# A fixed, software-pipelined order on three engines for the second part of a feed-forward up projection

## The chip, the cores and the metric

The kernel runs on one core of one Trainium2 chip. The metric is device time in microseconds (us) for one execution, median of the runs shown. Engines are called TensorE (PE in the profile), VectorE (DVE), ScalarE (ACT), GpSimd (POOL) and SyncE (SP, which here only issues transfers). A PE row has one matmul, a PEld row the loading of its weights.

## The reference

One decoder layer in fp32, 512 positions, model width 1024. A mixer comes first (mLSTM heads and a convolution group); the change concerns what follows it, the conditioned convolutional feed-forward network with 2816 hidden channels:

```python
mod = silu(c) @ ada_w + ada_b
sh1, sc1, g1, sh2, sc2, g2 = jnp.split(mod, 6)
...
u = rms_norm(x, ffn_pre_g) * (1.0 + sc2) + sh2
up = causal_dwconv(u @ ffn_up, ffn_conv_w, ffn_conv_b)   # width 3
a, gt = jnp.split(up, 2, axis=-1)
f = (silu(gt) * a) @ ffn_down
x = x + g2 * rms_norm(f, ffn_post_g)
```

## The kernel before

**Products in fp32.** Each fp32 operand is written as the sum of a high part (`h` at the end of a name), which ScalarE rounds off by a copy, and a low part (`l`), the remainder. A product is three matmuls: high by high, high by low, low by high (L188 to L190).

**The up projection** has 22 blocks of 128 hidden channels. A block has an "a" half and a "gate" half, and its weights are a tile of 128 x 2048, loaded by SP into a raw buffer; there are two raw buffers. Blocks 0 to 7 are multiplied plainly. From block 8 on blocks come in pairs, an even block i and the odd block j = i + 1; m = i / 2 counts pairs, m = 4 to 10.

*The even block* is computed with seven products of half size in place of eight (a Strassen-like scheme). Its weights are four quarters of 128 x 512 in the raw buffer: a11, a12, a21, a22, the quarters 0 to 3, each loaded by a DMA of 256 KB (L1064 to L1069). Seven operands are formed: p1 is a11, p2 is a12, p4 is a22; p5, p7, p6 and p3 are sums and differences, which VectorE makes in place (L1093, L1094, L1097 for the first three, L1118 for p3: it puts a12 - a11 into a11). p1, p5, p7 and p6 are multiplied first (`first_products`) into the PSUM banks `upx`, `upz` and `upw`. ScalarE then copies two products to SBUF (both called `p` in rows, L1106 and L1109) and VectorE makes four sums between banks (L1110 to L1113); p2, p3 and p4 are accumulated on top of these (L1086 holds all matmuls of the seven products, 84 of them for a block, 12 a product, each with 256 columns).

*The odd block* is multiplied plainly in two halves, 24 matmuls of 512 columns each (L188 to L190); its raw buffer is the second one.

**Two kinds of split.** `w_split` (p1, p5, p7, p6, p3): ScalarE copies the high part (L170), GpSimd subtracts to get the low part (L171). `added_split` (p2, p4, all quarters of odd blocks): ScalarE writes the high part (L1077) and its negative (L1078), and GpSimd issues a DMA (L1079) that adds the raw quarter to the negative, so that the low part is made by a transfer, which reads the raw buffer.

**What follows a block.** The convolution of width 3 (`conv3`): ScalarE takes the middle tap out of PSUM (L995), VectorE adds two more (L997). For the gate half ScalarE applies Silu (L1141), and VectorE multiplies (L1142) into F, one buffer for each pair. `forms` then prepares the pair's F as operand of the down projection, which uses the seven-product scheme too: four sums and differences on VectorE (L1021 to L1024), two splits by ScalarE and VectorE (L1013, L1014), and two DMAs issued by ScalarE that put the rest aside in DRAM (`g2d`, L1031, L1032). For the first four pairs, m = 0 to 3, the split operands go to DRAM as well ("spilled", `own_d`).

**Beside this**, eight pieces of the modulation (`ada`, 512 KB each) are loaded on ScalarE's queue and summed up on VectorE (L153, L155), two at a time at blocks 4, 8, 12 and 16 (`asides`).

**The down projection** runs over 11 groups, one for each pair, in the order 4 to 10, then the spilled 0 to 3; group numbers in rows (`b_3h`, `wd_1`) count in that order. A group's weights are loaded by SP (`load1`, L1220) into the two raw buffers and two more places (`wdmore`), combined on VectorE and split by ScalarE and VectorE (`forms1`, L1226 to L1230), and one combination is written back to DRAM (`t2d`). SP issues, in this order: the loads of groups 0, 1 and 2; sixteen reloads of spilled operands, 256 KB each (`reload`, L1188); then for each group its write of `t2d`, the load of the group three further on, and a load of what `forms` put aside (L1246).

**Who sets the order.** TensorE and SP work in the order in which the code is written. The instructions of ScalarE, VectorE and GpSimd are ordered by a scheduler of the language, by its own estimates of when data are ready, except inside `in_order()` (L70 to L82), where these three also keep the order of the code. The up projection from block 8 on is not inside such a region before the change.

## Time and profile before

| | |
|---|---|
| time, median of 3 runs | 826.61 us (826.61, 823.62, 826.79) |
| the profiled execution | 830.35 us |
| its span on the core | 828.6 us, mean granted TensorE clock 0.962 |
| bytes moved by DMA | 144.80 MB, mean 175 GB/s over the span |
| first product of block 8 on TensorE | at 506.2 us |
| first product of block 20 | at 675.0 us |
| 497 to 560 us: TensorE busy, granted clock, DMA share | 44.73 us of 63, 0.85, 0.70 |
| 560 to 705 us | 126.03 us of 145, 0.90, 0.62 |
| 705 to 828 us | 107.26 us of 123, 0.94, 0.76 |

The span is the time between the first and the last instruction on the core; the execution's own time has some 1.75 us around it. A row of the trace reads: start and length in us, engine, line, operation, output <- inputs, shapes, count, and in brackets how long the engine stood idle before it and what ended that. In a table by windows each engine has its busy time and, in brackets, its instructions, in the order PE, PEld, DVE, ACT, POOL; behind them stand the granted clock (1.00 is full speed), the busy share of the 16 DMA engines and GB/s. A row "PE upx <- DVE upx: 33.1, 6, 14.1" is the total of waits, their number and the longest.

### The profile page before, as it was taken

Reading aid. Unit: us, or ns where it says so; the run is one execution under the profiler, and the core shown is the slowest. Engines: PE = TensorE matmul, PEld = TensorE weight load, DVE = VectorE, ACT = ScalarE, POOL = GpSimd, SP = SyncE. Lnnn points to the kernel's source line nnn. Section 1 sums busy time; section 2 is a strip of 40 time slices with the busy share of each in tenths; the row PEclk is TensorE's granted clock in tenths of the full one; section 3 lists DMA queues with packets and bytes.
Section 4 is the critical chain, followed back from the end, with each engine's and each line's share of the span. In section 5 each row is a group of like instructions: output and inputs, shape, how many; then the busy total and the mean of one; then the engine's idle time right before and its main releaser. Section 6 shows DMA issues by size and latency. Waiting matters only on the chain.

```text
span 828.6 us, 11531 instructions
## 1 busy us (share of the span) xinstructions
PE 769.2 (93%) x3961; PEld 656.9 (79%) x3961; DVE 642.3 (78%) x1039; ACT 444.9 (54%) x846; POOL 372.9 (45%) x315
## 2 busy tenths in 40 slices
PE   7999999999999999999999999389798896879996
PEld 5788898788888889888899888379787796658885
DVE  6979999999999577378676997565676547479996
ACT  5555375867664566523354447265564654255762
POOL 1049495977986444538234765145453440000001
PEclk9999999999999999999999999598899997979998
DMA  9973223131234524287453456686775871797982
GB/s 332 382 267 103 102 97 107 52 102 51 79 125 150 180 78 156 99 294 269 175 182 136 142 190 153 215 181 121 209 171 159 195 152 48 227 372 249 307 282 101
DMA packets 53119, 144.80 MB, mean 175 GB/s; under 512 B 6050, under 2 KB 7490, under 8 KB 48964
## 3 DMA queue, kind: packets, MB, share of 16 engines
q1 hardware_dynamic: 32724, 100.37, 35.3%
q10 hardware_dynamic: 14288, 32.68, 11.3%
q0 software_dynamic: 6048, 11.01, 7.8%
q8 instruction: 31, 0.51, 0.2%
q14 instruction: 28, 0.23, 0.1%
HBM read 117.42 MB, written 15.61 MB: 161 GB/s over the span
## 4 chain that ended last, share of the span: by engine, by line
PE 56%; DVE 20%; DMA 10%; issue 6%; ACT 4%; POOL 2%; SPq 0%; ACTq 0%; DVEq 0%; POOLq 0%
DVE cv L731 10%; PE up L189 4%; PE up L190 4%; PE up L188 4%; PE p L1314 4%; PE upx L1086 4%; DMA wup_p4l<-wups 3%; PE glu L189 3%; PE glu L188 3%; PE glu L190 3%; DMA wups<-in_w_up 2%; PE glu L316 2%; PE p L189 2%; PE p L188 2%; PE p L190 2%
## 5 line engine op out<-in xcount | busy, mean ns | idle before, releaser
L731 DVE SCALAR_TENSOR_TENSOR cv<-gt,cvw,cv 128x505 f32<-128x505 f32 (+24 forms) x200 | 137.3, 729 | 2.3 <-ACT cv L719 1.1
L685 POOL TENSOR_TENSOR ro2r<-ro2t,mhalf 128x1 f32<-128x1 f32 x1 | 0.6, 561 | 134.5 <-DVE ro2t L683 134.5
L1086 PE MATMUL upx<-u2h,wup_p2h 128*128 128x256 f32 x28 | 11.3, 405 | 37.0 <-DVE upx L1113 33.1
L727 POOL TENSOR_TENSOR cs<-cs,cs 128x510 f32<-128x510 f32 (+3 forms) x32 | 41.9, 1309 | 0.3
L1086 PEld LDWEIGHTS upx<-u2h,wup_p2h 128*128 128x128 f32 x28 | 7.8, 280 | 39.8 <-ACT wup_p5h L170 14.5
L171 POOL TENSOR_TENSOR wup_p5l<-wups,wup_p5h 128x512 fp32r<-128x512 f32 x7 | 9.0, 1292 | 52.3 <-ACT wup_p5h L170 46.1
L155 DVE SCALAR_TENSOR_TENSOR junk<-ada,cb 128x1024 bf16<-128x1024 f32 x20 | 29.0, 1448 | 3.4 <-DMA ada<-in_adaT 3.3
L725 ACT ACTIVATE cs<-gt,cvw 128x511 f32<-128x511 f32 (+4 forms) x40 | 27.4, 716 | 6.2 <-POOL cs L727 3.0
L189 PE MATMUL up<-u2l,wup_0h 128*128 128x512 f32 (+1 forms) x72 | 25.7, 356 | 0.2 <-DVE u2l L910 0.2
L188 PE MATMUL up<-u2h,wup_0h 128*128 128x512 f32 (+1 forms) x72 | 25.6, 356 | 0.0
L190 PE MATMUL up<-u2h,wup_0l 128*128 128x512 f32 (+1 forms) x72 | 25.5, 354 | 0.0
L171 POOL TENSOR_TENSOR wqko_1024l<-wqko,wqko_1024h 128x512 fp32r<-128x512 f32 x12 | 15.5, 1293 | 18.3 <-ACT wqko_1024h L170 12.9
L171 POOL TENSOR_TENSOR wglu_0l<-wglu,wglu_0h 128x512 fp32r<-128x512 f32 x4 | 5.6, 1408 | 40.3 <-PE glu L190 40.2
L155 DVE SCALAR_TENSOR_TENSOR junk<-spare,cb 128x1024 bf16<-128x1024 f32 x12 | 19.2, 1598 | 3.4 <-DMA spare<-in_adaT 3.1
L1013 ACT ACTIVATE fh<-F 128x512 fp32r<-128x512 f32 x11 | 6.9, 628 | 27.3 <-DVE F L1022 14.1
L188 PE MATMUL qko<-uh,wqko_1024h 128*128 128x512 f32 x48 | 20.6, 430 | 0.0
L188 PE MATMUL qko<-uh,wqko_0h 128*128 128x512 f32 x48 | 20.2, 420 | 0.0
L276 DVE SCALAR_TENSOR_TENSOR junk<-ada,cb 128x1024 bf16<-128x1024 f32 x16 | 19.5, 1220 | 0.1
L171 POOL TENSOR_TENSOR wo_512l<-wo,wo_512h 128x512 fp32r<-128x512 f32 x8 | 12.9, 1617 | 13.4 <-ACT wo_512h L170 13.4
L190 PE MATMUL qko<-uh,wqko_1024l 128*128 128x512 f32 x48 | 18.8, 392 | 0.0
L171 POOL TENSOR_TENSOR wqko_0l<-wqko,wqko_0h 128x512 fp32r<-128x512 f32 x12 | 16.6, 1382 | 4.9 <-ACT wqko_0h L170 4.9
L190 PE MATMUL qko<-uh,wqko_0l 128*128 128x512 f32 x48 | 18.8, 391 | 0.0
(1207 smaller groups left out, 3186.8 us busy)
## 6 DMA issues: line engine op xcount, KB each, us to landing
wups<-in_w_up SPq DMA_DIRECT2D x56, 256.0 KB, 5.6
wqko<-in_w_qko SPq DMA_DIRECT2D x12, 1024.0 KB, 4.8
ada<-in_adaT ACTq DMA_DIRECT2D x20, 512.0 KB, 5.2
ada<-in_adaT SPq DMA_DIRECT2D x16, 512.0 KB, 7.4
wo<-in_w_out SPq DMA_DIRECT2D x8, 1024.0 KB, 4.8
wup<-in_w_up SPq DMA_DIRECT2D x8, 1024.0 KB, 5.0
spare<-in_adaT ACTq DMA_DIRECT2D x12, 512.0 KB, 7.2
wd<-in_w_down SPq DMA_DIRECT2D x6, 768.0 KB, 6.6
```

What stands on the lines that cost most here:

```text
L155: t = V.scalar_tensor_tensor(out=junk, in0=r, scalar=1.0, in1=cb, op0=ALU.mult, op1=ALU.mult, accum_out=mod[:, i : i + 1])
L171: (eng or G).tensor_tensor(out=lo[:, :n], in0=src, in1=hi[:, :n].bitcast(F32), op=ALU.subtract)
L188: PE.matmul(ps, a[0], b[0], start=start, stop=False)
L189: PE.matmul(ps, a[0], b[1], start=False, stop=False)
L190: PE.matmul(ps, a[1], b[0], start=False, stop=stop)
L276: V.scalar_tensor_tensor(out=junk, in0=first[k][:, i * D : (i + 1) * D], scalar=1.0, in1=cb, op0=ALU.mult, op1=ALU.mult, accum_out=part[k] ...
L316: PE.matmul(banks0[i], blk(wk, i)[a], u[k][b], start=k == 0 and a == b, stop=False)
L725: S.activation(t[:, d:], cvx[j][:, : T - d], AF.Copy, scale=w(CK - 1 - d))
L727: G.tensor_tensor(out=side[:, d:], in0=side[:, d:], in1=t[:, d:], op=ALU.add)
L731: last_tap[0] = V.scalar_tensor_tensor(out=cp[:, d:], in0=cvx[j][:, : T - d], scalar=w(CK - 1 - d), in1=cp[:, d:], op0=ALU.mult, op1=ALU.add)
L1086: PE.matmul(ps, x, y, start=start and k == 0 and n == 0, stop=stop and k == NT - 1 and n == 2, skip_group_check=True)
L1314: PE.matmul(ps[q], x, y, start=False, stop=m == NM - 1 and i == 2, skip_group_check=True)
```

## The change

The part of the up projection from block 8 on is written out inside an `in_order()` region, in one loop over pairs, so ScalarE, VectorE and GpSimd run it in the order of the code. The loop is pipelined over pairs. In the turn of pair m, the engines other than TensorE and SP do:

1. first half-convolution of the odd block of pair m - 1, then p2's split of block i;
2. Silu and product of that odd block; then p3's split (its difference now has a place of its own, `s4`) and p4's split;
3. `forms` of pair m - 1 (high parts and the DMAs), then the copies and sums between banks for block i, then the low parts of `forms` (`forms_low`);
4. the splits of the second half of odd block j;
5. the first forms (p1, p5, p7, p6) of block i + 2, with the first convolution of block j between them; then the splits of the first half of block j + 2;
6. the sums of two pieces of the modulation and the loads of the next two (pairs 4 to 7, before them two loads ahead of the loop);
7. the two convolutions of block i, its Silu and its product.

SP's loads for the next pair stand in the code behind p4's split: quarters 0 and 1 of block j + 2, then 2, 0, 1, 3 of block i + 2, and later 2 and 3 of block j + 2. Before, they were 0, 2, 3, 1 of an even block, then 0 to 3 of the odd one. The order of TensorE's instructions is the same as before. There are still two raw buffers.

The sixteen reloads are issued by GpSimd instead of SP.

Lines of the changed kernel that the prediction speaks of: L1077 to L1079 and L170, L171, L995, L997 as before; L1094 and L1098 (the in-place sums of `first_forms` for p5 and p6), L1115 to L1118 (sums between banks), L1137 (Silu), L1147 (sum of the modulation), L1274, L1284 and L1300 (the down projection's load, write of `t2d` and load of what was put aside).

The diff, cut to its core:

```diff
@@ forms
+        pairs.append([(slot(f"fh{m}_{n}", F32R), slot(f"fl{m}_{n}", F32R)) for n in range(2)])
+        for (hi, _), z in zip(pairs[m], (F[:, :T], ysum)):
+            S.activation(hi, z, AF.Copy)
...
+    def forms_low(m, F):
+        for (hi, lo), z in zip(pairs[m], (F[:, :T], ysum)):
+            V.tensor_tensor(out=lo, in0=z, in1=hi.bitcast(F32), op=ALU.subtract)
@@ first_forms
-        r = up_load(i, (0, 2, 3, 1))
+        a11, a21, a22 = (quarter(up_raw[i % 2], q) for q in (0, 2, 3))
...
         w.append(w_split(a21, f"wup{i}_p5"))
+        middle()
         w.append(w_split(a11, f"wup{i}_p7"))
@@ last_forms
-        V.tensor_tensor(out=a11, in0=a12, in1=a11, op=ALU.subtract)
-        return [added_split(a12, f"wup{i}_p2"), w_split(a11, f"wup{i}_p3"), added_split(a22, f"wup{i}_p4")]
@@ the loop over pairs, before
-            r, w = first_forms(i)
-            banks = first_products(i, w)
-            z = up_load(j, range(4))
-            pa = plain_half(cvbank(f"up{j}_0"), [added_split(quarter(z, q), f"wup{j}_{q}") for q in range(2)], 0)
-            ja = conv3(pa, j, f"fa{j}")
-            last_products_up(banks, last_forms(i, r))
-            unit_out(i, conv3(banks[0], i, f"fa{i}"), conv3(banks[1], NF + i, f"fg{i}"), F)
-            pg = plain_half(cvbank(f"up{j}_1"), [added_split(quarter(z, q), f"wup{j}_{q}") for q in range(2, 4)], 0)
-            unit_out(j, ja, conv3(pg, NF + j, f"fg{j}"), F)
@@ and now
+    up_load(2 * MS, (0, 2, 3, 1))
+    up_load(2 * MS + 1, range(4))
+    with in_order():
+        fetched = [ada_fetch(40 + n) for n in range(2)]
+        first_forms(2 * MS, lambda: None)
+        halves_w = [added_split(quarter(up_raw[1], q), f"wup{2 * MS + 1}_{q}") for q in range(2)]
...
+            if before is not None:
+                bj, ba, bg = before
+                fg = conv3(bg, NF + bj, f"fg{bj}")
+            V.tensor_tensor(out=s4, in0=a12, in1=quarter(up_raw[0], 0), op=ALU.subtract)
+            late = [added_split(a12, f"wup{i}_p2")]
+            if before is not None:
+                unit_out(bj, ba, fg, Fs[m - 1])
+            late.append(w_split(s4, f"wup{i}_p3"))
+            late.append(added_split(a22, f"wup{i}_p4"))
+            if m + 1 < NM:
+                up_load(j + 2, range(2))
+                up_load(i + 2, (2, 0, 1, 3))
+            if before is not None:
+                forms(m - 1, Fs[m - 1])
+            between(i, *banks)
+            if before is not None:
+                forms_low(m - 1, Fs[m - 1])
...
+            halves_w = [added_split(quarter(up_raw[1], q), f"wup{j}_{q}") for q in range(2, 4)]
+            if m + 1 < NM:
+                up_load(j + 2, range(2, 4))
...
+                first_forms(i + 2, value)
...
+            last_products_up(X, Z, late)
+            pg = plain_half(cvbank(f"up{j}_1"), halves_w, 0)
+            if m + 1 < NM:
+                halves_w = [added_split(quarter(up_raw[1], q), f"wup{j + 2}_{q}") for q in range(2)]
...
+            unit_out(i, conv3(X, i, f"fa{i}"), conv3(Z, NF + i, f"fg{i}"), Fs[m])
+            before = j, ja[0], pg
@@ reload
-                nc.sync.dma_start(z.bitcast(F32), own_d[m][:, (2 * n + e) * T : (2 * n + e + 1) * T])
+                G.dma_start(z.bitcast(F32), own_d[m][:, (2 * n + e) * T : (2 * n + e + 1) * T])
```

More of the change, by code (lines that the diff above doesn't have):

```diff
@@ L1068, in up_load @@
             nc.sync.dma_start(quarter(up_raw[i % 2], q), quarter(w_up[i], q))
-        return up_raw[i % 2]
     def quarter(r, b):
@@ L1086, in form_product, with first_forms @@
                 PE.matmul(ps, x, y, start=start and k == 0 and n == 0, stop=stop and k == NT - 1 and n == 2, skip_group_check=True)
-    def first_forms(i):
-        r = up_load(i, (0, 2, 3, 1))
-        a11, a21, a22 = quarter(r, 0), quarter(r, 2), quarter(r, 3)
-        w = [w_split(a11, f"wup{i}_p1")]
+    sforms = {}
+    def first_forms(i, middle):
+        a11, a21, a22 = (quarter(up_raw[i % 2], q) for q in (0, 2, 3))
+        w = sforms[i] = [w_split(a11, f"wup{i}_p1")]
         V.tensor_tensor(out=a11, in0=a11, in1=a21, op=ALU.subtract)
@@ L1111, in first_products, with last_products_up @@
         V.tensor_tensor(out=Z[:, :HT], in0=Z[:, :HT], in1=u2, op=ALU.add)
+        V.tensor_tensor(out=X[:, HT:], in0=X[:, HT:], in1=u2, op=ALU.add)
         V.tensor_tensor(out=Z[:, HT:], in0=Z[:, :HT], in1=p15[:, HT:], op=ALU.add)
-        V.tensor_tensor(out=X[:, HT:], in0=X[:, HT:], in1=u2, op=ALU.add)
-        return X, Z
-    def last_forms(i, r):
-        a11, a12, a22 = quarter(r, 0), quarter(r, 1), quarter(r, 3)
-        V.tensor_tensor(out=a11, in0=a12, in1=a11, op=ALU.subtract)
-        return [added_split(a12, f"wup{i}_p2"), w_split(a11, f"wup{i}_p3"), added_split(a22, f"wup{i}_p4")]
-    def last_products_up(banks, w):
-        X, Z = banks
+    def last_products_up(X, Z, w):
         form_product(X[:, :HT], w[0], B21, False, True)
@@ new lines, in own_out, with open_F @@
+    def own_out(m):
+        for n, pair in enumerate(pairs[m]):
+            for e, z in enumerate(pair):
+                nc.scalar.dma_start(own_d[m][:, (2 * n + e) * T : (2 * n + e + 1) * T], z.bitcast(F32))
+    g2 = []
+    MS = SUNITS[0] // 2
+    Fs = {}
+    def open_F(m):
+        Fs[m] = vpool.tile([P, 2 * T + 8], F32, tag="vh", name=f"F{m}")
+    for m in range(MS):
+        open_F(m)
+        for i in (2 * m, 2 * m + 1):
+            pa, pg = plain_unit(i)
+            unit_out(i, conv3(pa, i, f"fa{i}"), conv3(pg, NF + i, f"fg{i}"), Fs[m])
+            if i in (3, 4):
+                token_forms(i - 3)
+        forms(m, Fs[m])
+        forms_low(m, Fs[m])
+        if m < SPILLED:
+            own_out(m)
```

83 lines of the change are left out of this document (45 added, 38 removed).

## The prediction

> **What bounds the kernel now.** I read the page first, then who waits for whom on TensorE, then the chain that ended last. The page: the span, and TensorE busy in 93% of it, so time can only come out of the 7% in which it is idle and of stretches at a low clock.
>
> ```profile
> span 828.6 us, 11531 instructions
> PE 769.2 (93%) x3961; PEld 656.9 (79%) x3961; DVE 642.3 (78%) x1039; ACT 444.9 (54%) x846; POOL 372.9 (45%) x315
> ```
>
> The waits of TensorE (total, times, longest) put nearly all of it into the two places that the change touches: six waits in the up projection from block 8 on, for the sum of products that VectorE writes into `upx`, and one in the down projection for the first copy of weight group 3.
>
> ```profile
> PE upx L1086 <- DVE upx L1113: 33.1, 6, 14.1
> PE p L188 <- ACT b_3h L1013: 9.1, 1, 9.1
> ```
>
> The chain that ended last shows what lies behind the first (start, length):
>
> ```profile
> 571.53 6.62 DMA wup_p4l<-wups
> 578.21 5.15 DMA wups<-in_w_up
> ...
> 587.03 0.34 DVE upx L1113
> 587.50 5.09 PE upx L1086 x24
> 592.60 1.44 PE upz L1086 x12
> ```
>
> So a pair of blocks is not held by matmuls. Its last accumulating transfer (p4) reads the quarter a22 of the one raw buffer that even blocks have; only when it has landed may the next even block's a22 be loaded into that place; only then can VectorE add it (L1094), ScalarE copy p5, and so on to the next p4. I call "leg L" the way from GpSimd's issue of p4 to the next L1094, and "leg M" the way from L1094 to the p4 of the same block. Three turns of L, and the first and last L1094 of blocks 10 to 20:
>
> ```profile
> 512.89 0.91 POOL L1079 DMA_DIRECT2D wup_p4l<-wups  x1 [0.85 <-ACT wup_2h L1077]
> 620.13 1.07 POOL L1079 DMA_DIRECT2D wup_p4l<-wups  x1
> 647.25 1.07 POOL L1079 DMA_DIRECT2D wup_p4l<-wups  x1
> 523.00 0.69 DVE L1094 TENSOR_TENSOR wups<-wups 128x512 f32<-128x512 f32 x1 [0.75 <-DMA wups<-in_w_up]
> 608.28 0.69 DVE L1094 TENSOR_TENSOR wups<-wups 128x512 f32<-128x512 f32 x1
> 631.28 0.69 DVE L1094 TENSOR_TENSOR wups<-wups 128x512 f32<-128x512 f32 x1 [0.39 <-DMA wups<-in_w_up]
> 659.73 0.69 DVE L1094 TENSOR_TENSOR wups<-wups 128x512 f32<-128x512 f32 x1 [2.46 <-DMA wups<-in_w_up]
> ```
>
> L was 10.1, 11.2 and 12.5 us, mean 11.2. From 523.00 to 659.73 lie five turns, 27.3 us each; so M was 16.1 on average. This loop has no TensorE in it. L is p4's transfer, about 0.4 for SP, and the load; their times from issue to landing, in this order:
>
> ```profile
> DMA to landing us min/median/max: 4.4/6.6/7.6
> DMA to landing us min/median/max: 3.3/5.6/9.2
> ```
>
> **The change part by part.** *The loop.* The change keeps one raw buffer for even blocks, and L's parts with it: p4's transfer, then the load of a22. What changes is M, the work that ScalarE does in a fixed order between p5 and p4. Both kernels split block 12 while blocks 10 and 11 are finished (fa10, fg10: the convolutions of block 10's two halves; fg11: of block 11's second half). ScalarE before, up to p4 of block 12:
>
> ```order
> L995 ACTIVATE fa10c<-upx_5389,vec 128x512
> L1077 ACTIVATE wup_0h<-wups_5123 128x512
> L1078 ACTIVATE wup_0l<-wups_5123 128x512
> L1077 ACTIVATE wup_1h<-wups_5123 128x512
> L1078 ACTIVATE wup_1l<-wups_5123 128x512
> L1077 ACTIVATE wup_p2h<-wups_5122 128x512
> L1078 ACTIVATE wup_p2l<-wups_5122 128x512
> L995 ACTIVATE fg10c<-upz_5390,vec 128x512
> L170 ACTIVATE wup_p3h<-wups_5122 128x512
> L1077 ACTIVATE wup_p4h<-wups_5122 128x512
> L1078 ACTIVATE wup_p4l<-wups_5122 128x512
> ```
>
> And now, behind the four copies 0h to 1l (s_6 is the difference for p3):
>
> ```order
> L995 ACTIVATE fa10c<-upx_5380,vec 128x512
> L995 ACTIVATE fg10c<-upz_5381,vec 128x512
> L1137 ACTIVATE fg10c<-fg10c 128x512
> L995 ACTIVATE fg11c<-up_1_5577,vec 128x512
> L1077 ACTIVATE wup_p2h<-wups_5105 128x512
> L1078 ACTIVATE wup_p2l<-wups_5105 128x512
> L1137 ACTIVATE fg11c<-fg11c 128x512
> L170 ACTIVATE wup_p3h<-s_6_5707 128x512
> L1077 ACTIVATE wup_p4h<-wups_5105 128x512
> L1078 ACTIVATE wup_p4l<-wups_5105 128x512
> ```
>
> Two Silus (L1137) and one more convolution moved ahead of p4, and each Silu waits for VectorE's taps, with all of the next block's splits queued behind it. The new M is walked with these rows, of blocks 16 (splits) and 14 (convolution):
>
> ```profile
> 609.06 0.64 ACT L170 ACTIVATE wup_p5h<-wups 128x512 fp32r<-128x512 f32 x1 [0.23 <-DVE wups L1094]
> 613.07 0.63 ACT L170 ACTIVATE wup_p6h<-wups 128x512 fp32r<-128x512 f32 x1 [1.53 <-DVE wups L1097]
> 615.69 0.62 ACT L1077 ACTIVATE wup_p2h<-wups 128x512 fp32r<-128x512 f32 x1
> 617.39 0.77 ACT L995 ACTIVATE fg14c<-upz,vec 128x512 f32<-128x512 f32 x1
> 618.05 0.62 ACT L170 ACTIVATE wup_p3h<-wups 128x512 fp32r<-128x512 f32 x1
> 618.45 1.53 DVE L997 SCALAR_TENSOR_TENSOR fg14c<-upz,vec,fg14c 128x511 f32<-128x511 f32 x2
> 620.08 0.63 ACT L1141 ACTIVATE fg14c<-fg14c 128x512 f32<-128x512 f32 x1 [0.35 <-DVE fg14c L997]
> ```
>
> From L1094 to p5 0.8, p5 to p6 4.0 (GpSimd's two subtractions and VectorE's L1098 between), p6 and four copies 2.6: 7.4. Two convolutions, 0.66 each from start to start; the first one's taps begin 0.8 after it (its length is 0.77) and the taps of two halves take 2 x 1.53: Silu at 7.4 + 0.8 + 3.1 + 0.1 = 11.4. The convolution of fg11 starts 0.5 later, its taps 0.8 after that and end at 14.2, VectorE's difference for p3 takes 0.69 like L1094, p3 starts at 14.9, and from p3 to p4 the rows give 620.13 - 618.05 = 2.1. M = 17.0, so a turn is 17.0 + 11.2 = 28.2 us, 0.9 more than before; in the first three of the five turns, ScalarE also issues two loads of the modulation (an issue took 0.33 us at 704.61 below, on SP), for which I add 0.4. Everything else of the pair hides in it: the matmuls (12 of half width took 1.44 at 592.60; 84 of these and 48 twice as wide make 10.1 + 11.5 = 21.6), the copies of `p`, GpSimd's six transfers, and VectorE's two sums for the modulation (L1147), which now fall between L1098 and the taps, while ScalarE does its four copies.
>
> One price here can be doubted. p3's subtraction on GpSimd now falls beside VectorE's forms of F, which read two SBUF operands. In these rows such a pair did meet: VectorE's product took 2.05 us beside GpSimd's p1, where the like L1094 takes 0.69.
>
> ```profile
> 603.38 1.63 POOL L171 TENSOR_TENSOR wup_p1l<-wups,wup_p1h 128x512 fp32r<-128x512 f32 x1
> 603.52 2.05 DVE L1142 TENSOR_TENSOR F<-fa13c,fg13c 128x512 f32<-128x512 f32 x1 [1.34 <-ACT fg13c L1141]
> ```
>
> I take 0 for the loop, since there GpSimd started first and only VectorE waited; if VectorE is first, p3 waits for one of its operations, 0.7 at most, and five turns cost 3.5. The Trainium skill (SBUF — State Buffer, section Who interferes with whom) says that a VectorE instruction with two SBUF inputs and a GpSimd instruction that reads SBUF exclude each other, and that the later one waits; these rows agree, and by that rule the sum would be 3.5 us higher if VectorE always came first.
>
> *The first pair.* Before, ScalarE came late to the copies of `p` (L1106), because its queue held DMA issues that waited for loads; TensorE stood for 14.12 us.
>
> ```profile
> 509.42 0.63 ACT L1141 ACTIVATE fg6c<-fg6c 128x512 f32<-128x512 f32 x1
> ...
> 523.38 0.63 ACT L1013 ACTIVATE fh<-F 128x512 fp32r<-128x512 f32 x1 [6.75 <-DMA wups<-in_w_up]
> ...
> 530.02 0.38 ACT L1106 ACTIVATE p<-upx 128x256 f32<-128x256 f32 x1 [4.00 <-DMA g2d<-ysq]
> 532.15 0.55 PE L1086 MATMUL upx<-u2h,wup_p2h 128*128 128x256 f32 x1 [14.12 <-DVE upx L1113]
> ```
>
> Now both convolutions of block 7 stand directly behind that Silu and the two modulation loads are gone from there. By the lengths above: convolutions at 509.96 and 510.62; their taps from 510.75 to 513.8; Silu 513.9; the product to 515.2, four forms of half the width to 516.7; two low parts and the difference for p3, some 0.6 each, to 518.5; p3 at 518.6, p4's transfer 2.1 later at 520.7, `p` three copies later at 520.2, and TensorE 2.13 later (532.15 - 530.02), at 522.3: 9.8 earlier. But the loop starts from p4: before 512.89, now 520.7. Block 10's L1094 comes at 520.7 + 11.2 = 531.9, before 523.00. So the first pair's gain is spent: L1094 of block 20 falls at 531.9 + 5 x 28.2 + 3 x 0.4 = 674.1, where it was 659.73.
>
> *The end of the up projection.* Block 20's p4 has landed M + 6.6 (its median) = 23.6 us behind its L1094; the matmuls of p4 (1.44) and of the last half block (24 of 0.24, 5.8) follow: TensorE begins the down projection at about 674.1 + 31 = 705.
>
> *The reload of the spilled groups.* On SP, sixteen reloads stood ahead of the write of `t2d` and of group 3's load; they move to GpSimd. SP before:
>
> ```order
> L1188 DMA fh_0b<-own_4552 128x512
> L1188 DMA fl_0b<-own_4552 128x512
> L1188 DMA fh_1b<-own_4552 128x512
> L1188 DMA fl_1b<-own_4552 128x512
> L1230 DMA t2d_4538<-wd_0_6854 128x512
> L1220 DMA wdmore<-in_w_down 128x1536
> ```
>
> And now, from group 1's load on:
>
> ```order
> L1274 DMA wd_1_6863<-in_w_down 128x1536
> L1274 DMA wdmore<-in_w_down 128x1536
> L1284 DMA t2d_4538<-wd_0_6861 128x512
> L1274 DMA wdmore<-in_w_down 128x1536
> L1300 DMA g2kept<-g2d_4531 128x768
> ```
>
> The trace: group 2's load at 704.61, group 3's, behind the reloads, at 722.26, and TensorE idle until it is split.
>
> ```profile
> 704.61 0.33 SPq L1220 DMA_DIRECT2D wdmore<-in_w_down  x1
> ...
> 722.26 0.33 SPq L1220 DMA_DIRECT2D wdmore<-in_w_down  x1
> 730.78 0.79 PE L188 MATMUL p<-b_3h,fh 128*128 128x512 f32 x1 [9.14 <-ACT b_3h L1013]
> 738.73 0.39 PE L188 MATMUL p<-b_4h,fh 128*128 128x512 f32 x1
> 740.00:760.00 20.00, 20.00 (x90) 16.57 (x89) 19.36 (x33) 11.09 (x21) 0.00 (x0) 1.00 0.84 280
> ```
>
> The wait of 9.14 goes. Next late is VectorE: groups 0 to 3 are now split after the up projection instead of in its gaps. Group 0 is loaded when block 20's p4 has landed, 768 KB instead of 256 (I add 1.0 to L): L1094 + 17.0 + 12.2 = + 29.2. From there to group 4's first low part stand 46 VectorE instructions; the last row has 33 in 19.36 us, 0.587 each, so 27.0: + 56.2, and with 0.7 to the matmul + 56.9. TensorE begins group 4 at 674.1 + 56.9 = 731.0, before at 738.73: 7.7 us earlier. From there the stage is as before (TensorE busy 20.00 of 20). On GpSimd the sixteen issues take some 1.07 us each, 17 us, behind its last accumulation and ahead of nothing until the norm factors at the end; the reloaded groups are used as the last four of eleven. I take nothing for them.
>
> *Sum.* The profiled execution took 830.35, its span 828.6. 828.6 - 7.7 = 820.9, plus the same 1.75 around it 822.6; the median, 826.61, lies 3.74 below that execution: **819** us.
>
> **The rivals.** *Transfers land faster* (0.12). Loads are issued further apart, so L is near its least, 4.4 + 0.4 + 3.3 = 8.1: 5 x 3.1 = 15.5 us less, **803**. Against it: three L of 10 to 12.5, and the same bytes per pair. The Trainium skill (DMA: Bandwidth & Descriptors, section Anatomy of one DMA) gives 2.0 us plus bytes at 436 GB/s, 2.6 for 256 KB; estimated from that page, L would be 6.5 and the time about 795. The medians above are more than twice the page's figure.
>
> *L grows: slower* (0.12). The reload of a22 now stands on SP behind the loads of a11 and a12 and beside the accumulations of the odd block. From L = 12.8 on (1.5 more per turn) the gain is gone; at 13.6 the kernel is 0.5% slower, and a load of 8 us gives 15.0, 5 x 3.8 = 19 us, **838**. For it: one load of 9.2. Against it: five turns would all have to be bad ones.
>
> *The end gives nothing* (0.18). VectorE's 46 instructions meet sixteen reloads and three weight loads on the same DMA engines; if groups 0 to 3 arrive some 7 us later, TensorE begins group 4 where it did: **827**, no change.
>
> That the loop is broken altogether (a turn of 21.6 us, TensorE the bound, 5 x 6.6 = 33 us less, 786) I give nothing: a22 has one place.
>
> **How the numbers follow.** The forecast has 0.58; its own bounds (L 10.1 to 12.5, five turns, -5.5 to +6.5; p3 up to +3.5) leave it faster by over 0.5% (4.1 us, about what a measurement can tell from no change) in 0.46, the same in 0.11, slower in 0.01. Fast transfers add 0.12 to faster; the slow loop 0.12 to slower; the empty end 0.03, 0.13 and 0.02. Together 0.61, 0.24, 0.15. Range 806 to 830: it leaves out the slow loop and half of the fast one.
>
> **What would show it.** Right: L1094 every 28 us from about 532; TensorE at `upx` p2 first at 522; its waits for L1117 fewer but other waits, for transferred low parts, in their place; the up projection's end near 705; no wait for b_3h, group 4 at 731. Wrong: turns of 25 us or less, TensorE without idle time between blocks 10 and 20, or an end before 695.

## The result

The changed kernel takes 832.99 us (median of 5 runs, 831.57 to 836.26), the kernel before 825.66 us beside it (823.62 to 826.79): a ratio of 1.0095, 95% interval 1.0067 to 1.0123. It is slower by 0.95%, where 819 us were forecast. The profiled execution, the longest of the five, took 836.26 us with a span of 834.6, against 828.6 before: 6.0 us more, where 7.7 less were forecast.

### The profile page after: what moved, and what is told of

The parts are those of the page before. It is cut to its first block, busy times and chain, and to the rows that moved or that the text cites. A ratio compares the mean times of both kernels' runs of the same rounds, so it can differ in the third digit from the quotient of the medians.

```text
span 834.6 us, 11552 instructions
## 1 busy us (share of the span) xinstructions
PE 773.6 (93%) x3961; PEld 659.3 (79%) x3961; DVE 646.9 (78%) x1039; ACT 444.8 (53%) x846; POOL 382.4 (46%) x331
## 4 chain that ended last, share of the span: by engine, by line
PE 45%; DVE 29%; issue 11%; ACT 6%; POOL 4%; DMA 3%; ACTq 0%; POOLq 0%; SPq 0%; DVEq 0%
DVE cv L731 10%; PE p L1368 4%; PE glu L316 3%; PE glu L188 3%; PE glu L189 3%; PE glu L190 3%; PE p L188 2%; PE p L189 2%; PE p L190 2%; PE mixa L188 2%; PE mixa L190 2%; PE mixa L189 2%; PE mixb L190 2%; PE mixb L189 2%; PE mixb L188 2%
## 5 line engine op out<-in xcount | busy, mean ns | idle before, releaser
L725 ACT ACTIVATE cs<-gt,cvw 128x511 f32<-128x511 f32 (+4 forms) x40 | 27.5, 717 | 5.9 <-POOL cs L727 2.7
L189 PE MATMUL up<-u2l,wup_0h 128*128 128x512 f32 (+1 forms) x72 | 26.1, 363 | 0.2 <-DVE u2l L910 0.2
L170 ACT ACTIVATE wup_p5h<-wups 128x512 fp32r<-128x512 f32 x7 | 4.4, 632 | 40.4 <-DVE wups L1094 40.4
L171 POOL TENSOR_TENSOR wqko_1024l<-wqko,wqko_1024h 128x512 fp32r<-128x512 f32 x12 | 16.3, 1356 | 18.4 <-ACT wqko_1024h L170 12.9
L171 POOL TENSOR_TENSOR wglu_0l<-wglu,wglu_0h 128x512 fp32r<-128x512 f32 x4 | 5.6, 1389 | 41.1 <-ACT wglu_0h L170 41.1
L171 POOL TENSOR_TENSOR wup_p5l<-wups,wup_p5h 128x512 fp32r<-128x512 f32 x7 | 9.1, 1295 | 31.1 <-ACT wup_p5h L170 31.1
L1079 POOL DMA_DIRECT2D wup_p2l<-wups x7 | 6.1, 876 | 36.3 <-ACT wup_p2l L1078 23.0
L155 DVE SCALAR_TENSOR_TENSOR junk<-ada,cb 128x1024 bf16<-128x1024 f32 x12 | 19.5, 1621 | 3.3 <-DMA ada<-in_adaT 3.2
L190 PEld LDWEIGHTS up<-u2h,wup_0l 128*128 128x128 f32 x72 | 14.0, 194 | 8.6 <-DMA wup_0l<-wups 6.7
L276 DVE SCALAR_TENSOR_TENSOR junk<-ada,cb 128x1024 bf16<-128x1024 f32 x16 | 19.5, 1218 | 0.1
L171 POOL TENSOR_TENSOR wo_512l<-wo,wo_512h 128x512 fp32r<-128x512 f32 x8 | 12.9, 1615 | 13.3 <-PE mixa L190 11.1
L171 POOL TENSOR_TENSOR wqko_0l<-wqko,wqko_0h 128x512 fp32r<-128x512 f32 x12 | 16.6, 1382 | 4.9 <-ACT wqko_0h L170 4.8
```

Source lines behind the costliest of these rows:

```text
L155: t = V.scalar_tensor_tensor(out=junk, in0=r, scalar=1.0, in1=cb, op0=ALU.mult, op1=ALU.mult, accum_out=mod[:, i : i + 1])
L171: (eng or G).tensor_tensor(out=lo[:, :n], in0=src, in1=hi[:, :n].bitcast(F32), op=ALU.subtract)
L189: PE.matmul(ps, a[0], b[1], start=False, stop=False)
L190: PE.matmul(ps, a[1], b[0], start=False, stop=stop)
L276: V.scalar_tensor_tensor(out=junk, in0=first[k][:, i * D : (i + 1) * D], scalar=1.0, in1=cb, op0=ALU.mult, op1=ALU.mult, accum_out=part[k] ...
L725: S.activation(t[:, d:], cvx[j][:, : T - d], AF.Copy, scale=w(CK - 1 - d))
```

## The profile after

The page of the changed kernel: as many matmuls as before, and TensorE busy in the same share.

```profile
span 834.6 us, 11552 instructions
PE 773.6 (93%) x3961; PEld 659.3 (79%) x3961; DVE 646.9 (78%) x1039; ACT 444.8 (53%) x846; POOL 382.4 (46%) x331
```

The waits of TensorE after (total, times, longest). The wait of 9.1 for `b_3h` is gone; in its place stands one of 9.5 for the taps of block 21 (`fg21c`), and the waits for the sums between banks are spread over all pairs: none is above 5.2 us, where the longest before was 14.1.

```profile
PE upx L1086 <- DVE upx L1117: 25.3, 6, 5.2
PE p L188 <- DVE fg21c L997: 9.5, 1, 9.5
PE upx L1086 <- ACT wup_2h L1077: 5.4, 1, 5.4
PE up L190 <- DMA wup_0l<-wups: 5.3, 3, 2.5
```

The turns of the loop: L1094 of blocks 10, 12 and 20, p4's issue for blocks 8, 10, 12 and 20, and TensorE's p2 of blocks 8, 18 and 20.

```profile
531.27 0.69 DVE L1094 TENSOR_TENSOR wups<-wups 128x512 f32<-128x512 f32 x1 [2.40 <-DMA wups<-in_w_up]
561.51 0.69 DVE L1094 TENSOR_TENSOR wups<-wups 128x512 f32<-128x512 f32 x1 [3.81 <-DMA wups<-in_w_up]
676.82 0.69 DVE L1094 TENSOR_TENSOR wups<-wups 128x512 f32<-128x512 f32 x1
523.37 0.90 POOL L1079 DMA_DIRECT2D wup_p4l<-wups  x1 [0.28 <-ACT p L1114]
549.30 0.89 POOL L1079 DMA_DIRECT2D wup_p4l<-wups  x1
579.52 0.90 POOL L1079 DMA_DIRECT2D wup_p4l<-wups  x1
693.69 0.89 POOL L1079 DMA_DIRECT2D wup_p4l<-wups  x1
524.79 0.55 PE L1086 MATMUL upx<-u2h,wup_p2h 128*128 128x256 f32 x1 [4.91 <-DVE upx L1117]
669.11 0.55 PE L1086 MATMUL upx<-u2h,wup_p2h 128*128 128x256 f32 x1 [4.86 <-DVE upx L1117]
697.90 0.55 PE L1086 MATMUL upx<-u2h,wup_p2h 128*128 128x256 f32 x1 [5.39 <-ACT wup_2h L1077]
```

The loop came out much as it was walked: L1094 of block 10 at 531.27 (forecast 531.9), M = 18.0 us in its first turns (549.30 - 531.27), L = 12.2 in the first (561.51 - 549.30) and 11.6 on average, block 20's L1094 at 676.82 (forecast 674.1). Ahead of the first turn, from p4 of block 8 to L1094 of block 10, L was 7.9. In the first four turns L1094 waits for the load of a22; in the fifth it does not, and follows p1's low part. The last row's wait of 5.39 is put down to a copy of block 21, which p2 does not read; the sum that p2 does need (L1117) ended beside it, at 697.75.

The table of the kernel before has block 20's first product at 675.0; its row stands at 673.88. Nothing below uses it.

The seam to the down projection is where the sum broke. On SP, GpSimd, ScalarE, VectorE and TensorE, in this order: the last accumulation out of the odd raw buffer; group 1's load, which needs that buffer; the instructions that wait for this load; and the taps of blocks 20 and 21, which stand behind them.

```profile
700.10 0.89 POOL L1079 DMA_DIRECT2D wup_3l<-wups  x1 [0.40 <-issue]
707.54 0.33 SPq L1274 DMA_DIRECT2D wd<-in_w_down  x1
716.40 0.63 ACT L1013 ACTIVATE b_1h<-wd 128x512 fp32r<-128x512 f32 x1 [7.09 <-DMA wd<-in_w_down]
716.67 0.69 DVE L1280 TENSOR_TENSOR wd<-wd 128x512 f32<-128x512 f32 x1 [5.42 <-DMA fl_1b<-own]
717.28 0.74 DVE L997 SCALAR_TENSOR_TENSOR fg20c<-upz,vec,fg20c 128x510 f32<-128x510 f32 x1
722.20 0.74 DVE L997 SCALAR_TENSOR_TENSOR fg21c<-up,vec,fg21c 128x510 f32<-128x510 f32 x1
711.36 0.39 PE L188 MATMUL p<-b_0h,fh 128*128 128x512 f32 x1
723.09 0.77 PE L188 MATMUL p<-t_0h,fh 128*128 128x512 f32 x1 [9.53 <-DVE fg21c L997]
744.75 0.39 PE L188 MATMUL p<-b_4h,fh 128*128 128x512 f32 x1
```

The profile puts VectorE's 5.42 us down to a reload; ScalarE's row beside it names the transfer that both wait for, group 1's load. TensorE starts the down projection with b_0 at 711.36, but three matmuls into its second product (t_0) it needs the PSUM bank that `fg21c` is read out of, and that read is queued behind a weight load. Group 4 begins at 744.75; before, at 738.73. From there to the end of the span it is 89.8 us, before 89.9: the whole difference of 6.0 us is there by group 4.

## The experiments

Theory A: the loss lies at the seam and in the loop, the loop's turn is L + M through the one raw buffer, and the reload's move is worth its 9 us. Rivals: (B) the reloads disturb the weight loads; (C) at the seam the weights are late anyhow; (D) the sums between banks set the turn; later (E) the succession of steps itself, a chain of hand-overs between engines, sets it; (F) the seam alone is the loss. The table has, from each trace, TensorE's p2 of blocks 8, 18 and 20 and the first product of group 4 (us), the mean turn (block 18 less block 8, over five), the median, and the ratio to the kernel before on the same chip with its interval. The columns up to group 4 are from one execution each, and a kernel's executions lie several us apart (the changed kernel: 831.6 to 836.3, e12: 827.5 to 835.9), so a difference of 2 or 3 us at group 4 says little. The medians are from different chips; the ratios are the fairer comparison.

| run | block 8 | block 18 | turn | block 20 | group 4 | median | ratio |
|---|---|---|---|---|---|---|---|
| before | 532.15 | 662.56 | 26.1 | 692.03 | 738.73 | 825.66 | |
| after | 524.79 | 669.11 | 28.9 | 697.90 | 744.75 | 832.99 | 1.0095 (1.0067 to 1.0123) |
| e1 | 526.54 | 668.75 | 28.4 | 697.50 | 749.55 | 840.75 | 1.0156 (1.0118 to 1.0194) |
| e2 | 530.80 | 658.92 | 25.6 | 689.27 | 723.02 | 817.08 | 0.9871 (0.9830 to 0.9913) |
| e3 | 524.76 | 669.49 | 28.9 | 698.28 | 744.95 | 833.43 | 1.0074 (1.0043 to 1.0105) |
| e4 | 523.58 | 658.19 | 26.9 | 687.78 | 734.16 | 825.07 | 0.9974 (0.9949 to 1.0000) |
| e5 | 523.51 | 664.73 | 28.2 | 699.87 | 739.01 | 830.28 | 1.0024 (0.9996 to 1.0052) |
| e6 | 535.30 | 664.17 | 25.8 | 699.42 | 743.66 | 835.57 | 1.0088 (1.0057 to 1.0119) |
| e7 | 534.64 | 663.71 | 25.8 | 705.88 | 739.82 | 832.24 | 1.0061 (1.0041 to 1.0080) |
| e8 | 521.59 | 660.25 | 27.7 | 685.01 | 737.62 | 829.69 | 1.0020 (0.9991 to 1.0049) |
| e10 | 528.87 | 675.39 | 29.3 | 702.77 | 737.70 | 829.28 | 1.0005 (0.9969 to 1.0040) |
| e11 | 536.14 | 661.08 | 25.0 | 693.98 | 740.52 | 831.80 | 1.0052 (1.0016 to 1.0087) |
| e9 | 527.77 | 655.24 | 25.5 | 682.60 | 725.60 | 817.10 | 0.9878 (0.9802 to 0.9953) |
| e12 | 525.49 | 668.26 | 28.6 | 694.14 | 738.07 | 832.00 | 1.0041 (1.0011 to 1.0071) |
| e14 | 523.04 | 666.17 | 28.6 | 692.08 | 737.56 | 831.76 | 1.0041 (1.0014 to 1.0068) |
| e13 | 528.20 | 656.16 | 25.6 | 680.99 | 719.35 | 814.43 | 0.9843 (0.9804 to 0.9881) |
| e15 | 528.47 | 656.20 | 25.5 | 680.95 | 721.77 | 813.33 | 0.9850 (0.9809 to 0.9890) |
| e16 | 527.44 | 647.02 | 23.9 | 670.17 | 714.85 | 806.86 | 0.9768 (0.9717 to 0.9819) |

### The reload alone: e1 and e2

In the kernel before (e2), and undone in the changed one (e1):

```diff
-                nc.sync.dma_start(z.bitcast(F32), own_d[m]...)
+                G.dma_start(z.bitcast(F32), own_d[m]...)
```

> The changed kernel with the sixteen reloads issued by SP again. Theory A (the reload's move is worth the 9.14 us wait for b_3h, and the loss comes from the up projection's end and from VectorE's queue standing before group 1's load): a wait of TensorE for group 3 comes back, 4 to 9 us, so 836 to 842 us against 833. Theory B (the sixteen reloads on GpSimd run beside the loads of groups 1 to 3, stretch them, and are the loss): group 1's load lands in 5 us and not in 9, and the time falls to 824 to 828.

> The kernel before with nothing changed but the queue of the sixteen reloads (GpSimd in place of SP). Theory A: the 9.14 us wait for b_3h goes, 7 to 9 us faster than before, 817 to 819. Theory B (the reloads disturb the weight loads): no gain, 825 to 830.

Both fell as theory A had them. In e2 TensorE meets no wait above 0.5 us between block 21 and group 4; in e1 the wait for group 3 is back.

```profile
PE p L188 <- ACT b_3h L1013: 6.5, 1, 6.5
PE p L188 <- DVE fg21c L997: 4.8, 1, 4.8
707.07 0.33 SPq L1274 DMA_DIRECT2D wd<-in_w_down  x1
711.16 0.63 ACT L1013 ACTIVATE b_1h<-wd 128x512 fp32r<-128x512 f32 x1 [2.10 <-DMA wd<-in_w_down]
```

Theory B is out as to the total, but half of it held. Group 1's load is issued at about the same moment in both kernels (707.07 and 707.54); in e1, without reloads beside it, the first copy of it starts 4.1 us after the issue, and in the changed kernel 8.9 us after (716.40 - 707.54). The wait for `fg21c` is 4.8 us in place of 9.5. So by these two traces about half of that wait comes from the reloads beside the load. Reloads that GpSimd issues behind group 1's load were not tried. With the reload on GpSimd in both, the rest of the change costs 833.0 against 817.1 us (ratios 1.0095 and 0.9871); with it on SP in both, e1 stands 1.56% above before.

### The queue at the seam alone: e3

```diff
+        if m == 1:                        # forms of group 1
+            for ins in traced[mark:]:     # behind block 21's Silu and product
...
+                tc.add_manual_dep(ins, end.ins.name, ...)
```

> The changed kernel, with group 1's forms of the down projection queued behind the last product of block 21 on VectorE and ScalarE. Theory A (TensorE's 9.53 us wait before the down projection is the queue order: the taps of block 21 stand behind an instruction that waits for group 1's load): TensorE begins group 0 at about 716 and not 723, and 4 to 7 us are gained, 826 to 829. Rival C (the weights are late anyhow): TensorE starts earlier but then waits as long for b_1h, no gain, 832 to 834.

Rival C held. TensorE's rows of e3:

```profile
714.77 0.47 PE L188 MATMUL p<-t_0h,fh 128*128 128x512 f32 x1 [1.46 <-DVE fg21c L997]
721.44 0.50 PE L189 MATMUL p<-b_1l,fh 128*128 128x512 f32 x1 [2.80 <-DVE b_1l L1014]
728.06 0.80 PE L189 MATMUL p<-t_1l,fh 128*128 128x512 f32 x1 [4.22 <-DVE t_1l L1014]
744.95 0.39 PE L188 MATMUL p<-b_4h,fh 128*128 128x512 f32 x1
```

The wait of 9.5 is gone, and group 4 begins where it did: the weights of group 1 are late themselves, and VectorE has their forms still to do.

### The transfer of p4: e4

```diff
-            late.append(added_split(a22, f"wup{i}_p4"))
+            late.append(w_split(a22, f"wup{i}_p4"))
```

> The changed kernel, with p4's low part made by a subtraction on GpSimd (1.3 us) in place of the accumulating transfer (6.9 us from issue to landing), so that the place of a22 comes free about 5 us earlier in each pair. Theory A (the turn is leg L plus leg M): turns of 24 us in place of 29, block 20's L1094 some 23 us earlier, 808 to 813. Rival D (the turn is set by the sums between banks and TensorE's waits for them, not by a22): turns stay at 28 to 29 us, 830 to 834.

Between the two: the turn falls by 2.0 us, not by 5. L1094 no longer waits for a load; it follows L1093, which waits for p1's low part on GpSimd, and that stands behind the copies and splits of the written order.

```profile
582.07 0.69 DVE L1093 TENSOR_TENSOR wups<-wups 128x512 f32<-128x512 f32 x1 [2.08 <-POOL wup_p1l L171]
582.79 0.69 DVE L1094 TENSOR_TENSOR wups<-wups 128x512 f32<-128x512 f32 x1
```

So the loop through a22 set the turn (in four of the five turns, by the waits above), but a second one, through the written order, lies only 2 us below.

### The last half block early: e5; the last forms early: e6 and e7

e5 moves one line, in the last turn alone; e6 takes p4, p2 and p3 into the first forms; e7 is both.

```diff
 # e5
+            if m == NM - 1:
+                halves_w = [added_split(quarter(up_raw[1], q), ...) for q in range(2, 4)]
             late = [added_split(a12, f"wup{i}_p2")]
 # e6, in first_forms
         w.append(w_split(a11, f"wup{i}_p6"))
+        w.append(added_split(a22, f"wup{i}_p4"))
+        w.append(added_split(a12, f"wup{i}_p2"))
+        V.tensor_tensor(out=s4, in0=a12, in1=a11, op=ALU.subtract)
+        w.append(w_split(s4, f"wup{i}_p3"))
```

> The changed kernel; in the last turn alone, the second half of block 21 is split ahead of p2 of block 20 instead of behind the sums between banks. Theory A (the end is set by group 1's load, which waits for the raw buffer of block 21, and by VectorE's work behind it): the load is issued 8 us earlier, VectorE's 5.4 us of waiting for it go, and 4 to 6 us are gained, 827 to 829. Rival: the load is late because of the sixteen reloads beside it, and an earlier issue gives 0 to 1 us, 832 to 833.

> The changed kernel, with p4, p2 and p3 split directly behind p6 in the first forms (and the next even block loaded as soon as its buffer is free), so that the single buffer's quarters come free some 12 us earlier in a turn. Theory A (the turn of 29 us is a loop through the one raw buffer of even blocks: a22 by p4's transfer, a11 by the difference for p3): turns of 22 to 25 us, 805 to 813. Rival D (the sums between banks and TensorE's waits for them set the turn): turns of 28 us or more, 828 to 835.

> The two edits together (the last forms early in every turn, and the second half of block 21 early in the last turn). Theory A: the gains add, 4 to 6 us below the run with the first edit alone, 800 to 808. If the end is set by something else: the same as that run.

e5 came to 830.3 where 827 to 829 were expected (the ratio fell by 0.7%, from 1.0095 to 1.0024): groups 0 and 1 were loaded earlier, and the scheduler put group 0's first sum ahead of the sums between banks of block 20, so the same wait moved there.

```profile
698.36 0.69 DVE L1283 TENSOR_TENSOR wd<-wd 128x512 f32<-128x512 f32 x1 [4.52 <-DMA wd<-in_w_down]
698.97 0.43 DVE L1116 TENSOR_TENSOR upz<-upz,u 128x256 f32<-128x256 f32 x1
699.87 0.55 PE L1086 MATMUL upx<-u2h,wup_p2h 128*128 128x256 f32 x1 [11.19 <-DVE upx L1117]
```

e6 is the miss that taught most. No L1094 waits for a load, and its turns did fall, but less than the table's 25.8 says, because that mean starts at block 8's late p2: L1094 of blocks 10 to 20 comes every 28.1 us, against 29.1 in the changed kernel. And the first pair came 10.5 us later (the added copies stand ahead of block 9's first half on ScalarE), and the last pair took 35.3 us in place of 28.8, since the sums between banks of block 20 were late:

```profile
699.42 0.58 PE L1086 MATMUL upx<-u2h,wup_p2h 128*128 128x256 f32 x1 [8.49 <-DVE upx L1122]
```

e7 only moved the wait again (p2 of block 20 at 705.88).

### The sums between banks: e8

```diff
             late = [added_split(a12, f"wup{i}_p2")]
+            between(i, *banks)
```

> The changed kernel, with the copies and sums between banks put behind p2's split, ahead of the Silu of the last odd block, in every turn. Theory A: TensorE's waits for L1117 (25 us in all) shrink to a few, but the turn does not get shorter; two more copies stand ahead of p4, so 29.5 to 30 us a turn, and 829 to 836 in all. Rival D (those waits are what the loop costs): the turn falls by the wait, 4 to 5 us, and the time to 810 to 818.

The total fits A, its mechanism does not: turns became 1.1 us shorter (28.86 and 27.73), not longer. M stayed as it was, 18.0 and then 16.9 (the copies fell into ScalarE's waits), and L shrank from 11.6 to 10.2 on average, most in the last two turns (8.4 and 9.7), where L1094 follows p1's low part and not a load. That this is because the sums no longer stand ahead of p1 is argued from the order. Rival D is out: the waits for L1117 went, and others took their place; block 20's p2 came 12.9 us earlier, and TensorE then waited 6.91 for the low part of block 21's second half and 6.95 for `fg21c`.

```profile
698.23 0.80 PE L190 MATMUL up<-u2h,wup_2l 128*128 128x512 f32 x1 [6.91 <-DMA wup_2l<-wups]
715.10 0.77 PE L188 MATMUL p<-t_0h,fh 128*128 128x512 f32 x1 [6.95 <-DVE fg21c L997]
```

### Another order in the loop: e10, e11, e9

e10 drops the region (`if True:` for `with in_order():`); e11 adds to e6 p1's split ahead of block j's second half; e9 writes another order: p2, p3 and p4 in the turn of p1 to p6, p4 by subtraction, the odd block's second half first, the next pair's loads earlier and in the old order, and copies of other blocks put into each wait of ScalarE. The cut shows one turn of e9, several lines of the code on one.

```diff
 # e9, a turn in its order
+            fg = conv3(bg, NF + bj, f"fg{bj}");  halves_w = halves_of_odd(j, range(2, 4))
+            unit_out(bj, ba, fg, Fs[m - 1]);  split1(i + 2);  forms(m - 1, Fs[m - 1])
+            sum1();  between(i, *banks);  sum2();  split57(i + 2);  forms_low(m - 1, Fs[m - 1])
+            split6(i + 2);  ja = conv3(pa, j, f"fa{j}")
+            halves_w = halves_of_odd(j + 2, range(2));  split2(i + 2)
+            fai, fgi = conv3(X, i, f"fa{i}"), conv3(Z, NF + i, f"fg{i}")
+            split34(i + 2);  unit_out(i, fai, fgi, Fs[m]);  split4(i + 2)
```

> The changed kernel with everything in place (pipelined code, the place of its own for p3's difference, the loads' order, the reload on GpSimd), but the region is no longer kept in the order of the code: the scheduler orders ScalarE, VectorE and GpSimd. Theory E (the written order itself is the loop: one turn is a chain of hand-overs between ScalarE, VectorE and GpSimd of 27 us, whatever the transfers do): turns come down, and with the reload's 9 us kept the time is 812 to 822. Rival (the pipelined shape of the code or its loads cost the time, not the order): 828 or more.

> The kernel of the run with p4, p2 and p3 early (835.6 us), with one more move: p1's split ahead of the four copies of block j's second half. In that kernel no step of the turn waits for a transfer, and its turn was still 27 us. Theory E (the turn is the chain of the written order): the chain loses the four copies and two issues ahead of p1, some 3 us, so turns of 24 us and 817 to 823. Theory A (a transfer through the raw buffer sets the turn): nothing changes, or a wait for a11 comes in its place, 833 to 838.

> The changed kernel with another written order: p4 by subtraction and p2, p3, p4 of the next even block split in the same turn as p1 to p6, and each wait of ScalarE for VectorE's taps or GpSimd's low parts filled with copies of another block; the second half of the odd block is split first in every turn. Theory E: the chain of hand-overs falls under TensorE's 21.6 us; turns of 22 to 24 us, group 1's weights loaded 20 us earlier, 790 to 803. Theory A alone: turns of 24 to 25 us, 805 to 812. Neither (a bound that is not in the order): 825 or more.

e10 fell on the rival's side (829.3, where 828 or more was given): keeping an order is not by itself what costs, since the scheduler's own order of the same code turns in 29.3 us at TensorE. Its splits did come faster (L1094 every 26.9 us), but its sums between banks came late, and TensorE waited 8.0 and 7.7 us for them in two turns. What it did mend is the seam (1.0 us of wait for `fg21c`). e11 shortened the turn by 0.8, not by 3 (L1094: 28.1 to 27.5). e9 turns in 25.5 by either count, 3.4 less than the changed kernel, and gains 16 us (ratio 0.9878 against 1.0095); the forecast for it, 22 to 24, was too bold. It holds e4's edit, which alone gave 2.0 us a turn, and the earlier loads; e9's order with p4's transfer kept was not tried, so how much the order itself gives is open.

### The seam mended: e12 to e15; the best order: e16

e12 is the changed kernel with only its last turn altered (e5's and e8's edits, in that turn) and the forms of group 0 behind block 20, group 1 behind block 21, and the later groups one behind the other; e14 is the same for groups 0 to 3 only. e13 and e15 put these queues behind e9's order. e16 adds to e15:

```diff
             split1(i + 2)
+            between(i, *banks);  sum1();  sum2();  split57(i + 2)
             forms(m - 1, Fs[m - 1])
-            sum1();  between(i, *banks);  sum2();  split57(i + 2)
```

> The changed kernel with its seven turns as they are (block 20's L1094 near 676), and only the end rewritten: in the last turn block 21's second half is split first and the sums between banks come behind p2's split, and on VectorE and ScalarE the forms of the down projection's groups stand behind the last products of blocks 20 and 21, group by group. Theory F (the loss of the change is at the end: what the last pair does late, and instructions that wait for weight loads standing ahead of it in VectorE's and ScalarE's queues): TensorE starts p2 of block 20 at 690 to 692 instead of 698, meets no long wait before the down projection, group 4 begins near 730, 818 to 822 us. Theory A/E (the loss is the loop: block 20 comes 17 us later than before): 828 or more.

> The run with the end alone rewritten (832.0 us, group 4 at 738.1, but 93.2 us from there to the end of the span against 89.9 in the changed kernel), with the order of groups enforced for groups 0 to 3 only. If the enforced order of the later groups cost those 3.3 us: group 4 again near 738, 826 to 829 us, so that mending the end is worth about 5 to 7 us of the change and the loop the rest. If the end is worth nothing: 832 or more.

> The interleaved order (817.1 us, turns of 25.5 us) with the same ordering of the down projection's groups behind blocks 20 and 21. Theory F: TensorE's waits of 6.1 us at p2 of block 20 and 6.1 us at the first group go, 804 to 810 us. If VectorE's work behind the up projection is the bound there: 814 to 818.

> The interleaved order with groups 0 to 3 kept behind blocks 20 and 21, and the later groups free (the run with all groups in order: 814.4 us, group 4 at 719.4, 94 us from there to the end). By the same account 809 to 812 us; if the later groups' order is not what cost the 4 us, 814 or more.

> As the run before, with one more move in every turn: the copies and sums between banks and the splits of p5 and p7 ahead of the forms of the last pair. Theory E (the turn is the chain of hand-overs in the written order): ScalarE's waits of 2.6 us for F and 2.3 us for the sum of p5, and TensorE's 3 to 4 us at p2, go; turns of 22 to 23 us in place of 25.5, 792 to 800 us. If the turn is already bound by TensorE or a transfer: 808 to 813, no change against the run before.

In e12 and e14 group 4 comes at 738.07 and 737.56, 6.7 and 7.2 us earlier than in the changed kernel, and the loop turns as slowly as it did. The ratio falls from 1.0095 to 1.0041, which is 4.5 us, with intervals that just meet (the medians, from other chips, lie 1 us apart, and the changed kernel's trace is of its longest execution). So the seam was worth some 4 to 7 us by the ratio and the traces, less by the medians, and F as the whole loss is out. e12 missed the 818 to 822 of theory F, and e14 the 826 to 829. Whether the later groups' order matters, the medians of e12 and e14 (832.0 and 831.8) and of e13 and e15 (814.4 and 813.3) do not tell apart; in the traces the stretch from group 4 to the end is 93.2 and 93.9 us in e12 and e13, which order them, and 89.8 in e14 and e15. e13 was expected at 804 to 810 by theory F, the seam's waits costing what they show, and fell on the side of its rival, VectorE's work behind the up projection (814 to 818); e15 lies between its two forecasts. e16's turns are 23.9 us with the same order on TensorE and the same two raw buffers (and p4's low part by subtraction, as in e9), and it is the fastest kernel here, 806.86 us, 2.3% below the kernel before. Its rows, p2 of blocks 18 and 20 and group 4:

```profile
647.02 0.35 PE L1086 MATMUL upx<-u2h,wup_p2h 128*128 128x256 f32 x1 [1.98 <-DVE upx L1117]
670.17 0.36 PE L1086 MATMUL upx<-u2h,wup_p2h 128*128 128x256 f32 x1 [1.93 <-DVE upx L1117]
704.09 0.80 PE L189 MATMUL p<-t_2l,fh 128*128 128x512 f32 x1 [4.12 <-DVE t_2l L1014]
714.85 0.39 PE L188 MATMUL p<-b_4h,fh 128*128 128x512 f32 x1
```

The forecast for it (792 to 800) failed by 1 to 2 us in each turn and at the seam again: the forms of four groups are still done behind the up projection, and TensorE waits for them.

## Why the prediction was wrong

**The reload: right, with a price left out.** No wait for `b_3h`; e2 has that edit alone, at 0.9871. But "I take nothing for them" does not hold in the changed kernel, where the reloads lie beside group 1's load: 8.9 us to its first copy, and 4.1 in e1.

**The first pair: a right number by luck.** L1094 of block 10 came at 531.27 (forecast 531.9), but out of two errors that cancel. p4 was issued at 523.37, not at 520.7: p3's split began at 521.10 in place of 518.6, behind five issues of writes to DRAM on ScalarE (518.64 to 521.00), four of them of the spilled pair, which the walk left out. And L was 7.9 there, not 11.2. p2 of block 8, at 524.79, was 2.5 late (522.3).

**The loop's turn: right in its parts.** L averaged 11.6 (11.2), M was 18.0, 18.0, 18.0, 16.9, 16.9 (17.4 and 17.0). The price that was in doubt came out as taken: in these turns p3's subtraction took some 1.3 us, and VectorE's first form waited beside it (1.43 us at 578.30, 0.42 alone). The missed 0.6 of the first three: ScalarE's loads of the modulation wait for the buffer that VectorE's second sum reads, and that sum took 2.19 us beside GpSimd's p6 (the first one 1.22); the convolution stands behind them.

```profile
596.78 2.19 DVE L1147 SCALAR_TENSOR_TENSOR junk<-ada,cb 128x1024 bf16<-128x1024 f32 x1
599.01 0.34 ACTq L1142 DMA_DIRECT2D ada<-in_adaT  x1
599.40 0.78 ACT L995 ACTIVATE fa12c<-upx,vec 128x512 f32<-128x512 f32 x1 [1.05 <-DVE junk L1147]
```

**The turn before: mis-sized.** The 27.3 us were a mean over five turns of which the first, from 523.00 to 556.96, still held the first pair's stall. The four others, 556.96 to 659.73, took 25.7 on average.

```profile
556.96 0.69 DVE L1094 TENSOR_TENSOR wups<-wups 128x512 f32<-128x512 f32 x1 [1.31 <-DMA wups<-in_w_up]
```

So the change does not add 0.9 us a turn but about 3. By p2 of blocks 8 and 18, as in the table, it is 28.9 against 26.1. This did not alter the sum, which was made with absolute times, but it hid that the change makes the loop worse, and that the first pair's gain of 7.4 is lost nearly twice over.

**The end of the up projection: failed.** "TensorE begins the down projection at about 674.1 + 31 = 705" took p4's landing as the last thing to wait for. But the sums between banks stand behind p4, two Silus and the forms in the written order, so p2 began at 697.90, and p2, p3 and p4 all had to follow, p2 and p3 at a granted clock of 0.50 (below). b_0 began at 711.36: 2.7 us of this from the loop, 3.7 from here.

**Next late is VectorE: failed, the larger error.** The sum let group 0's load start the work and VectorE's instructions follow without a gap, and gave TensorE's own way no price. VectorE's work was sized well: from group 0's first sum at 704.96 to `b_4l` it ran the 46 instructions, 27.2 us busy (forecast 27.0) and 5.9 idle, 5.4 of this for group 1's load. But it was not what TensorE met last: `b_4l` was done at 738.12, 6.6 us before group 4 began.

```profile
737.44 0.68 DVE L1014 TENSOR_TENSOR b_4l<-wd,b_4h 128x512 fp32r<-128x512 f32 x1
```

In fact group 1's load, issued at 707.54 because block 21's second half is split last (before, both were issued by 683.74, and the first low part of group 1 was done 24 us earlier), was what the instructions waited for that stood in VectorE's and ScalarE's queues ahead of the taps of blocks 20 and 21, and it took longer beside the reloads. TensorE's way is 711.36, 2.2 for its first nine matmuls, the wait of 9.53, and 21.7 for the rest of four groups, 1.9 of it because the first nine matmuls behind the wait start 0.43 us apart and not 0.23: 744.75. With the forecast's 705 and no wait it would have been about 726.9, 4.1 ahead of VectorE's 731.0. So 6.4 + 9.5 + 1.9 - 4.1 = 13.7 us, the whole miss at group 4. The rows before, for the last line:

```profile
678.51 5.23 SPq L1220 DMA_DIRECT2D wd<-in_w_down  x2
693.66 0.68 DVE L1014 TENSOR_TENSOR b_1l<-wd,b_1h 128x512 fp32r<-128x512 f32 x1
```

e3 shows that this wait and VectorE's late weights were tied: taking away the first alone gains nothing. e12 and e14, which also bring the loads forward, gain 6.7 to 7.2.

**The rivals.** "The end gives nothing" named the right place, and reloads and weight loads did meet there, but not that it could cost; L hardly grew (11.6), and transfers were not faster. None ended at 833. The estimate of 6.5 for L out of the Trainium skill's fit (DMA: Bandwidth & Descriptors, section Anatomy of one DMA) does not follow from it: the section gives that fit for transfers issued from GpSimd, which only one of L's two transfers is, and 2.6 + 0.4 + 2.6 make 5.6; measured, L was 11.6.

**Against the old order with the reload on GpSimd (e2)** group 4 comes 21.7 us later: 6.0 us earlier at the first p2, 16.2 later over five turns, 1.6 gained in the last pair, and 13.1 lost between block 20's p2 and group 4. Most edits leave that last stretch at 43 to 53 us (e9 43.0, e16 44.7, e8 52.6). It is 38.4 in e13, 39.1 in e5 and 40.8 in e15, and e7 (33.9) and e10 (34.9) come to e2's 33.75, but only because p2 of block 20 is late in them: their group 4 is no earlier than 737. That e2 has both, an early p2 and a short stretch, because groups 0 and 1 are split in VectorE's gaps around block 20's p2 (`b_0l` at 683.82, `b_1l` at 690.95, p2 at 689.27) is argued from its rows, not shown by a run.

**What sets the turn** is shown in part: without p4's transfer it is 26.9, with the last forms early 25.8 (28.1 by L1094), with other successions and without p4's transfer 25.5 and 23.9, and 29.3 where the scheduler orders the pipelined code. So a22's loop bound the changed kernel's turn, and close below it a chain of hand-overs. Which links bind in e16 was not tried; in its trace L1094's counterpart (L1188) of blocks 12, 14 and 16 again waits 1.2 to 1.4 us for a load.

```profile
576.49 0.69 DVE L1188 TENSOR_TENSOR wups<-wups 128x512 f32<-128x512 f32 x1 [1.40 <-DMA wups<-in_w_up]
```

## What to carry to other kernels

At the seam between two stages, list for each engine's queue which instruction waits for the next stage's first load and what of the old stage stands behind it; a load that waits for the old stage's last buffer, put ahead of the work that frees a PSUM bank, stalls the bound engine whatever the loop before it gains. When a forecast rests on a turn, take the turn before from the steady turns only, and compare both kernels at the same instruction of the bound engine. When the one loop that you see is cut, the next may lie 2 us below; price it before expecting more. And check a forecast leg by leg: a sum that comes out can hold two errors that cancel.
